# One streaming-encoder step on one core: the heads' weights loaded early, their magnitudes summed with ln_pre in the matmul, and prepared one step ahead

## The chip, the core and the metric

The kernel runs on one core of a Trainium2 chip. The metric is the device time of one execution in microseconds (us). Engines are named as the profile names them: PE is TensorE (PEld its weight loads), DVE is VectorE, ACT is ScalarE, POOL is GpSimd, SP is SyncE, which here issues the DMAs. TensorE's clock has two levels, 1.2 and 2.4 GHz; the profile's PEclk column says which share of 2.4 GHz was granted (0.5 is 1.2 GHz).

## What is computed

One layer is applied to a prompt of 4096 tokens and to a sample of 32 tokens of a running stream (model width 1024).

```
h    = RMSNorm(x) * ln_pre
proj = h @ w_in          # columns: B_a | C_a | X_a | Z_a | qkv (1536) | Z_g (512) | a_dec, b_beta (8)
q,k,v = silu(conv4_causal(qkv));  q, k L2-normalised per head (4 heads x 128)
S_t  = exp(g_t) (I - beta_t k_t k_t^T) S_{t-1} + beta_t k_t v_t^T ;  o_t = q_t^T S_t / sqrt(128)
y_g  = RMSNorm_head(o) * silu(Z_g);   y_a = B_a * conv3_causal(C_a * X_a) * silu(Z_a)
y    = x + RMSNorm_post(concat(y_a, y_g) @ w_out) * ln_post
```

## The kernel before, in words

Matmuls run on f16 pairs (a high and a low part; three products replace one f32 product). A weight column tile `ct` is 128 columns of `w_in`: 0 to 15 belong to group A, 16 to 31 to the heads (q 16 to 19, k 20 to 23, v 24 to 27, Z_g 28 to 31), and 32 holds the eight gate columns. Each tile is prepared once: it is loaded (512 KB), multiplied by `ln_pre` (line 182), its absolute values (184) are summed over the rows by eight matmuls with a matrix of ones (190), a power of two per column follows from the sum (193 to 200), the tile is scaled by it (202), and split into the high part on ACT (651) and the low part on POOL or DVE (652). Two tiles, a pair, are prepared together by `prep_b`.

The program has three stages: the heads with the sequential recurrence (to about 1320 us), group A by a Winograd scheme (to about 2000 us) and the output projection. The heads' stage goes over 16 blocks of 256 tokens; the sample goes with block 0. A block takes the eight pairs in the order k, k, q, q, v, v, z, z (`steps`); each is a projection (388 to 390, `pjs_...` for the sample, `pj_...` for the block), and for q, k and v a convolution with three DVE instructions per tile (405). Weights of the heads are prepared during block 0, the pair of a step in that step (from step 5 on, `AS`, one step ahead). Group A's tiles are prepared during the later blocks by `prep_a`, which runs after `subst` of its block, a chain of small POOL instructions (495 to 500) whose result `merge` needs (546) for the block's recurrence.

The order of the instructions on each engine's queue is set when the program is built, by a scheduler with its own clock; each queue then runs strictly in that order, and the loads of SP likewise. Tiles are loaded into a ring of five buffers, `xt`, which the loads of `x` share (k tiles go to rooms `v` and `zg`, which only later blocks fill). A load waits until its buffer's last reader is done.

Of the kernel before, what the change touches and what calls it, by code (L numbers as in the profile page):

```python
# [10 lines left out]
BF16 = mybir.dt.bfloat16  # L11
F32 = mybir.dt.float32
I32 = mybir.dt.int32
AF = mybir.ActivationFunctionType
ALU = mybir.AluOpType
# [3 lines left out]
P = 128  # L19
D = 1024  # L20
KT = D // P
NH = 4
NB1 = 256
# [9 lines left out]
NXT = 5  # L33
# [1 line left out]
LS = 2  # L35
XPE = 256
AH = 1
AS = 5
VLN = (20,)
VLO = (21,)  # L40

# [1 line left out]
def bc(ap, axis, n):  # L43

    shape = list(ap.shape)
    shape.insert(axis, n)
    return ap.unsqueeze(axis).to_broadcast(shape)
# [3 lines left out]
def hybrid_kernel(  # L51
# [11 lines left out]
    dma = nc.sync.dma_start  # L63
# [89 lines left out]
    def bank(tag, shape, nm):  # L153
        return pp.tile(shape, F32, tag=tag, bufs=1 if tag in "om" else 2, name=f"{tag}{nm}")
# [7 lines left out]
    def te(shape, dtype, tag, bufs=1, nm=""):  # L162
        return pe.tile(shape, dtype, tag=tag, bufs=bufs, name=f"{tag}{nm}")

    def tl(shape, dtype, tag, bufs=1, nm=""):
        return pl.tile(shape, dtype, tag=tag, bufs=bufs, name=f"{tag}{nm}")

    def scaled(cts, n=P, urow=None):


        ws = []
        first = cts[0] >= 16
        nm = f"{cts[0]}"
        L = bank("r" if first else "g", [P, 2, P], f"L{nm}")[:, :len(cts), :n]
        for i, ct in enumerate(cts):
            if 20 <= ct < 24:
                w = tl([P, D], F32, "v" if ct < 22 else "zg", 2, f"w{ct}")
            else:
                w = te([P, D], F32, "xt", NXT, f"w{ct}")
            w = w.rearrange("p (k c) -> p k c", k=KT)[:, :, :n]  # L180
            dma(w, w_in[:, ct * P:ct * P + n].rearrange("(k p) c -> p k c", p=P))
            (V if ct in VLN or not first else G).tensor_tensor(w, w, bc(lnp, 2, n), ALU.mult)
            ab = te([P, D], BF16, "jb", 1, f"w{ct}").rearrange("p (k c) -> p k c", k=KT)[:, :, :n]
            A.activation(ab, w, AF.Abs)
            kn = KT
            if not first:
                for kn in (4, 2, 1):
                    V.tensor_tensor(ab[:, 0:kn], ab[:, 0:kn], ab[:, kn:2 * kn], ALU.add)
            for k in range(kn):
                T.matmul(L[:, i], ones16, ab[:, k, :], start=k == 0, stop=k == kn - 1)  # L190
            ws.append(w)
        e = te([P, 2, P], I32, "we", 1, nm)[:, :len(cts), :n]
        V.tensor_scalar(e.bitcast(F32), L, 2.0 ** -100, None, ALU.max)
        V.tensor_scalar(e, e, EXP_MASK, None, ALU.bitwise_and)
        if urow is not None:
            V.tensor_scalar(urow.bitcast(I32), e[:, 0], 1, float(-(WS + HS) * BIT), ALU.mult, ALU.add)
        else:
            u = te([1, 2, P], I32, "wu", 1, nm)
            V.tensor_scalar(u, e[0:1], 1, float(-(WS + HS) * BIT), ALU.mult, ALU.add)
        V.tensor_scalar(e, e, -1, float((254 + WS) * BIT), ALU.mult, ALU.add)  # L200
        for i, w in enumerate(ws):
            V.tensor_tensor(w, w, bc(e[:, i].bitcast(F32), 1, KT), ALU.mult)
        if urow is None:
            up = bank("o" if first else "g", [P, 2], f"u{nm}")
            for i in range(2):
                T.matmul(up[:, i:i + 1], u[:, i].bitcast(F32), one1, start=True, stop=True)
            V.tensor_copy(usc[:, cts[0]:cts[0] + 2], up)
        return ws


    order = {"exp": None, "silu": None}
# [501 lines left out]
    smp = blocks1[0]  # L713
    groups[SG].insert(0, smp)
    xprep(groups[0][0])

    cst = te([P, 2, P], I32, "we", 1, "cst")[:48, 0].bitcast(F32)
    dma(cst, conv_qkv_w[0].rearrange("j (c p) -> (j c) p", p=P))
# [48 lines left out]
    for gi, grp in enumerate(groups):  # L767
        for b in grp:
            setup_block(b)
            if b["s"]:  # L770
                b["hist"] = te([P, 12, 3], F32, "hists", 2, "i")
                if gi:
                    for c in range(0, 12, 2):
                        init_hist(b, 16 + c)
                state[1] = te([P, NH, P], F32, "hl", 4, "s0")
                dma(state[1], state_gdn[0, 0].rearrange("h k v -> k h v"))
            elif gi:
                b["hist"] = groups[gi - 1][-1]["hist_new"]
        for si, (kind, c0) in enumerate(steps):
            if gi == 0 and si == 4:  # L780
                in_turn([gates(b) for b in grp])
                for b in grp:
                    decays(b)
            if gi == 0:
                for kd_, c_ in steps[:si + 1 + (AH if si >= AS else 0)]:
                    ct = (28 if kd_ == "z" else 16) + c_
                    if ct not in W:
                        prep_b(ct)
                if kind != "z":
                    init_hist(smp, 16 + c0)  # L790
            for b in grp:
                n = b["n"]
                if kind == "z":
                    z_pair(b, c0)
                elif kind == "v":
                    qkv_pair(b, c0, b["v"][:, c0 - 8:c0 - 6, :n])
                else:
                    h0 = c0 % 4
                    qkv_pair(b, c0, b["qk"][:, h0:h0 + 2, 0 if kind == "k" else 1, :n])
            finish(prevs, si)  # L800
            if si == (2 if gi else 6) and gi + 1 < len(groups):
                for b in groups[gi + 1]:
                    xprep(b)
            s1 = 4 if gi + LS < len(groups) else 3
            if si in (s1, s1 + 1):
                for b in grp:
                    if si - s1 < b["nch"]:
                        stage1(b, si - s1)
            if si == s1 + 1:
                for b in grp:  # L810
                    rnorms(b)
                    subst(b)
            if si == (3 if gi else 7) and gi + 1 < len(groups):
                in_turn([gates(b) for b in groups[gi + 1]])
            if si == 6 and 1 <= gi <= 13 or si == 2 and gi in (4, 7, 10):

                p = grp[-1] if si == 6 else prevs[-1]
                with tc.issue_after(p["stage1_end"]), tc.issue_after(p["subst_end"]):
                    prep_a()
        if gi + 1 < len(groups):  # L820
            for b in groups[gi + 1]:
                decays(b)
        for b in grp:
            if b["last"]:
                out_hist(b)
        prevs = grp
# [426 lines left out]
```

## Time and profile before

| | us |
|---|---|
| median of 3 runs (lowest, highest) | 2398.5 (2389.68, 2398.57) |
| profiled execution, its own time | 2393.51 |
| its span in the profile | 2391.8 |
| PE busy in the span | 2156.4 (90%) |
| DVE, ACT, POOL busy | 1699.0 (71%), 992.5 (41%), 1195.2 (50%) |
| mean granted clock of PE | 0.962 |

Busy shares are means over the whole span. Stretch by stretch the picture differs: PE is busy 53 to 60 us of nearly every 60 from 240 us on, and a third to three quarters of it before, during block 0. A "releaser" in a row is what ended the idle time of an engine. Times in the profile are counted from the span's start.

### The profile page before, as it was taken

Reading aid. Unit: us, or ns where it says so; the run is one execution under the profiler, and the core shown is the slowest. Engines: PE = TensorE matmul, PEld = TensorE weight load, DVE = VectorE, ACT = ScalarE, POOL = GpSimd, SP = SyncE. Lnnn points to the kernel's source line nnn. Section 1 sums busy time; section 2 is a strip of 40 time slices with the busy share of each in tenths; the row PEclk is TensorE's granted clock in tenths of the full one; section 3 lists DMA queues with packets and bytes.
Section 4 is the critical chain, followed back from the end, with each engine's and each line's share of the span. In section 5 each row is a group of like instructions: output and inputs, shape, how many; then the busy total and the mean of one; then the engine's idle time right before and its main releaser. Section 6 shows DMA issues by size and latency. Waiting matters only on the chain. (4 is left out here: it accounts for less than half of the span.)

```text
span 2391.8 us, 48652 instructions
## 1 busy us (share of the span) xinstructions
PE 2156.4 (90%) x18626; PEld 1706.8 (71%) x18626; DVE 1699.0 (71%) x4666; ACT 992.5 (41%) x2497; POOL 1195.2 (50%) x1581
## 2 busy tenths in 40 slices
PE   3677989899999999999999799899999999999998
PEld 3566877778777777787778678788888887444443
DVE  4886878987689888786777675676575565666763
ACT  4454656565666566555654220222121121433321
POOL 3526246752575644454454740766456611554542
PEclk9888999999999999999989899999999999999999
DMA  6334333534333442244324304311211133443431
GB/s 117 53 93 106 80 75 96 116 82 92 92 100 78 109 112 75 68 91 118 70 72 125 101 24 174 104 66 54 80 59 39 54 100 98 136 150 115 157 115 54
DMA packets 296913, 221.39 MB, mean 93 GB/s; under 512 B 166392, under 2 KB 236856, under 8 KB 296680
## 3 DMA queue, kind: packets, MB, share of 16 engines
q1 hardware_dynamic: 296680, 218.28, 33.5%
q8 instruction: 146, 2.39, 0.4%
q14 instruction: 87, 0.71, 0.1%
HBM read 127.84 MB, written 74.64 MB: 85 GB/s over the span
## 5 line engine op out<-in xcount | busy, mean ns | idle before, releaser
L388 PE MATMUL pj_c<-hhi,w 128*128 128x256 f16 x1536 | 429.3, 280 | 1.2 <-DMA hhi<-xth 1.2
L390 PE MATMUL pj_c<-hhi,w 128*128 128x256 f16 x1536 | 429.7, 280 | 0.0
L389 PE MATMUL pj_c<-hlo,w 128*128 128x256 f16 x1536 | 428.9, 279 | 0.0
L867 PEld LDWEIGHTS <-w_a 128*128 128x128 f16 x2880 | 269.9, 99 | 59.5 <-issue 25.6
L1130 PEld LDWEIGHTS <-opm 128*128 128x128 f16 x1536 | 149.6, 98 | 189.8 <-issue 15.5
L500 POOL TENSOR_TENSOR lt<-lt 128x112 f32<-128x112 f32 (+29 forms) x496 | 250.0, 504 | 38.9
L495 POOL TENSOR_TENSOR la<-la,lt 128x1024 f32<-128x1024 f32 x16 | 38.7, 2421 | 449.9 <-DVE lt L490 270.9
L390 PEld LDWEIGHTS <-w 128*128 128x128 f16 x2176 | 215.5, 100 | 53.2 <-POOL w L652 23.0
L499 POOL TENSOR_TENSOR lt<-la,lt 128x112 f32<-128x112 f32 (+29 forms) x496 | 233.1, 470 | 38.8
L388 PEld LDWEIGHTS <-w 128*128 128x128 f16 x2176 | 215.8, 100 | 34.1 <-issue 2.1
L389 PEld LDWEIGHTS <-w 128*128 128x128 f16 x2176 | 215.7, 100 | 30.7 <-issue 0.5
L405 DVE SCALAR_TENSOR_TENSOR qk<-u,cw,qk 128x256 f32<-128x256 f32 x384 | 214.9, 596 | 9.0 <-ACT qk L403 8.4
L867 PE MATMUL pja<-op,w_a 128*128 128x256 f16 x1536 | 194.5, 276 | 7.0 <-DVE w L881 3.4
L1079 POOL TENSOR_TENSOR mab<-mab 128x1024 bf16<-128x1024 bf16 (+2 forms) x48 | 103.6, 2159 | 130.8 <-ACT mab L1077 128.4
L867 PE MATMUL ga<-op,w_a 128*128 128x256 f16 x1152 | 149.8, 275 | 14.0 <-DVE w L881 8.1
L389 PE MATMUL pj_z<-hlo,w 128*128 128x256 f16 x512 | 144.6, 282 | 0.0
L390 PE MATMUL pj_z<-hhi,w 128*128 128x256 f16 x512 | 144.4, 282 | 0.0
L388 PE MATMUL pj_z<-hhi,w 128*128 128x256 f16 x512 | 144.3, 282 | 0.0
L1130 PE MATMUL pjo<-w_o,opm 128*128 128x512 f16 x528 | 118.2, 379 | 3.8 <-DVE v13y L1154 2.0
L1130 PE MATMUL ro<-w_o,opm 128*128 128x512 f16 x504 | 114.7, 383 | 3.9 <-DVE v7y L1154 2.0
L881 DVE TENSOR_TENSOR w<-pja,w 128x256 f32<-128x256 f32 x168 | 67.4, 420 | 70.6 <-PE pja L867 68.0
L1130 PE MATMUL go<-w_o,opm 128*128 128x512 f16 x504 | 112.7, 379 | 3.9 <-DVE v19y L1154 2.0
(707 smaller groups left out, 4946.5 us busy)
## 6 DMA issues: line engine op xcount, KB each, us to landing
xt<-in_x_prompt_dram SPq DMA_DIRECT2D x32, 512.0 KB
op<-hTd SPq DMA_DIRECT2D x32, 512.0 KB
mx<-mxd SPq DMA_DIRECT2D x16, 1024.0 KB
xtw<-in_w_in_dram SPq DMA_DIRECT2D x28, 512.0 KB
wad<-hl SPq DMA_DIRECT2D x56, 256.0 KB
gB<-gd SPq DMA_DIRECT2D x16, 516.0 KB
hTd<-hhi SPq DMA_DIRECT2D x16, 512.0 KB
hTd<-hlo SPq DMA_DIRECT2D x16, 512.0 KB
```

The lines of the kernel that those rows point to most:

```text
L388: T.matmul(pt[:, i, :n], wh[:, k, :], b["hi"][:, k, :n], start=k == 0, stop=False)
L389: T.matmul(pt[:, i, :n], wh[:, k, :], b["lo"][:, k, :n], start=False, stop=False)
L390: T.matmul(pt[:, i, :n], wl[:, k, :], b["hi"][:, k, :n], start=False, stop=k == KT - 1)
L405: V.scalar_tensor_tensor(d, u[:, i, j:j + n], cw[:, j, c0 + i:c0 + i + 1], d, ALU.mult, ALU.add)
L495: E.tensor_tensor(la, la, bc(rl, 1, 32), ALU.mult)
L499: E.tensor_tensor(tm, bc(la[:, j, j + 1:32], 2, w), bc(lt[:, j, 0:w], 1, r), ALU.mult)
L500: last = E.tensor_tensor(lt[:, j + 1:32, 0:w], lt[:, j + 1:32, 0:w], tm, ALU.subtract)
L867: T.matmul(out, lt(x, k), rh(y, k), start=start and k == n == 0, stop=stop and k == 3 and n == 2)
L881: V.tensor_tensor(dst, p, src, ALU.add)
L1079: G.tensor_tensor(ab[:, 0:m], ab[:, 0:m], ab[:, m:2 * m], ALU.add)
L1130: T.matmul(p, mo[:, x, k, t * P:t * P + m], WO[y, k][:, hf * 512:hf * 512 + 512], start=k == i == 0, stop=k == KT - 1 and i == 2)
```

## The change

- The ten tiles of the heads that are first in order (20 to 23, 16 to 19) and, two steps ahead, the others get a function `stage` that only issues the load. Tiles 16 and 17 go to a buffer of the tag `qk`, tile 18 to `la`, the gate columns to `hl`, tiles 19 and 24 on to the ring `xt`; tiles 20 to 23 stay in `v` and `zg`.
- For the heads' tiles the absolute values are taken from the weight as loaded, and the eight matmuls use the absolute values of `ln_pre`, spread to 128 columns (`lnab`, one ACT instruction at the start), as the left operand instead of ones. The multiplication by `ln_pre` stays, but the sum no longer waits for it. The absolute values go to two buffers (`o`) instead of one (`jb`).
- Pairs are prepared one step ahead from the first step (`AS` is gone), and loaded one more step ahead.
- For group A's 16 tiles the multiplication by `ln_pre` moves from DVE to POOL.

```diff
+    def stage(ct, n=P):
+        nm = f"w{ct}"
+        if ct in (20, 21, 22, 23):
+            w = tl([P, D], F32, "v" if ct < 22 else "zg", 2, nm)
+        elif ct in (16, 17):
+            if ct == 16:
+                staged["qk"] = tl([P, NH, 2, NB1], F32, "qk", 3, nm).rearrange("p h x n -> p (h x n)")
+            w = staged["qk"][:, (ct - 16) * D:(ct - 15) * D]
+        elif ct == 18:
+            w = tl([P, 32, 32], F32, "la", 1, nm).rearrange("p a b -> p (a b)")
+        elif n < P:
+            w = te([P, KT * n], F32, "hl", 4, nm)
+        else:
+            w = te([P, D], F32, "xt", NXT, nm)
+        w = w.rearrange("p (k c) -> p k c", k=KT)
+        dma(w, w_in[:, ct * P:ct * P + n].rearrange("(k p) c -> p k c", p=P))
+        staged[ct] = w
...
-            (V if ct in VLN or not first else G).tensor_tensor(w, w, bc(lnp, 2, n), ALU.mult)
-            ab = te([P, D], BF16, "jb", 1, f"w{ct}").rearrange("p (k c) -> p k c", k=KT)[:, :, :n]
-            A.activation(ab, w, AF.Abs)
...
+            w = staged.pop(ct)
+            if first:
+                ab = tl([P, D], BF16, "o", 2, f"w{ct}").rearrange("p (k c) -> p k c", k=KT)[:, :, :n]
+                A.activation(ab, w, AF.Abs)
+                (V if ct in VLN else G).tensor_tensor(w, w, bc(lnp, 2, n), ALU.mult)
+                for k in range(KT):
+                    T.matmul(L[:, i], lnab[:, k], ab[:, k, :], start=k == 0, stop=k == KT - 1)
             else:
+                G.tensor_tensor(w, w, bc(lnp, 2, n), ALU.mult)
...
+    lnab = tl([P, KT, P], BF16, "vn", 1, "lnab")
+    A.activation(lnab, bc(lnp, 2, P), AF.Abs)
...
     xprep(groups[0][0])
+    for ct in (20, 21):
+        stage(ct)
...
+    for ct in (22, 23, 16, 17, 18, 19):
+        stage(ct)
+    prep_b(22)
...
-                for kd_, c_ in steps[:si + 1 + (AH if si >= AS else 0)]:
-                    ct = (28 if kd_ == "z" else 16) + c_
+                cts = [(28 if kd_ == "z" else 16) + c_ for kd_, c_ in steps]
+                for ct in cts[:si + 1 + AH]:
                     if ct not in W:
                         prep_b(ct)
+                for ct in cts[si + 1 + AH:si + 2 + AH]:
+                    if ct not in staged:
+                        stage(ct)
+                        stage(ct + 1)
```

What this does to the queues shows in three places. On SP, at the start of the program, the kernel before issues the loads of `x` (xt), small constants (nea, dtb, gwc), the gate columns (xtw_302) and only then the second pair of k tiles:

```order
L235 DMA xt_0_238<-in_x_prompt_dram 128x1024
L235 DMA xt_128_241<-in_x_prompt_dram 128x1024
L731 DMA nea<-in_a_log_dram 128x4
L734 DMA dtb<-in_dt_bias_dram 128x4
L735 DMA gwc<-in_gdn_norm_w_dram 128x1
L181 DMA xtw_302<-in_w_in_dram 128x8x8
L776 DMA hls_332<-in_state_gdn_dram 128x4x128
L181 DMA zgw_468<-in_w_in_dram 128x8x128
L181 DMA zgw_481<-in_w_in_dram 128x8x128
L181 DMA xtw_643<-in_w_in_dram 128x8x128
```

The changed kernel, at the same place of SP's queue:

```order
L261 DMA xt_0_240<-in_x_prompt_dram 128x1024
L261 DMA xt_128_243<-in_x_prompt_dram 128x1024
L185 DMA zgw_290<-in_w_in_dram 128x8x128
L185 DMA zgw_292<-in_w_in_dram 128x8x128
L185 DMA qkw_294<-in_w_in_dram 128x8x128 x2
L185 DMA law_297<-in_w_in_dram 128x8x128
L185 DMA xtw_299<-in_w_in_dram 128x8x128
L762 DMA nea<-in_a_log_dram 128x4
L765 DMA dtb<-in_dt_bias_dram 128x4
L766 DMA gwc<-in_gdn_norm_w_dram 128x1
L185 DMA hlw_359<-in_w_in_dram 128x8x8
```

Six tile loads (22, 23, 16 to 19) moved ahead of the constants and of the gate columns, which are now hlw_359. On ACT, in block 0's first step, the kernel before takes the gate columns' absolute values (jbw_305) early, and the copies of the transposed x (hhi_235) come some rows later:

```order
L184 ACTIVATE jbw_305<-xtw_302 128x8x8
L184 ACTIVATE jbw_471<-zgw_468 128x1024
L651 ACTIVATE w_20_226<-vw_188 128x1024
L184 ACTIVATE jbw_484<-zgw_481 128x1024
L651 ACTIVATE w_21_230<-vw_201 128x1024
L248 ACTIVATE xt_0_238<-xt_0_238,xss_237 128x1024
L248 ACTIVATE xt_128_241<-xt_128_241,xss_237 128x1024
L184 ACTIVATE jbw_646<-xtw_643 128x1024
L253 ACTIVATE hhi_235<-gx_0_0_257 128x4x128
```

The changed kernel, the same stretch of ACT's queue:

```order
L274 ACTIVATE xt_128_243<-xt_128_243,xss_239 128x1024
L763 ACTIVATE nea<-nea 128x4
L202 ACTIVATE ow_361<-hlw_359 128x8x8
L202 ACTIVATE ow_525<-qkw_294 128x1024
L279 ACTIVATE hhi_237<-gx_0_0_259 128x4x128
L677 ACTIVATE w_22_336<-zgw_290 128x1024
L279 ACTIVATE hhi_237<-gx_0_1_266 128x4x128
L202 ACTIVATE ow_536<-qkw_294 128x1024
L677 ACTIVATE w_23_340<-zgw_292 128x1024
```

The gate columns (ow_361) now stand behind the scaling of x and directly ahead of x's copies. On POOL, the kernel before multiplies four further tiles by `ln_pre` before the first low part (w_20_227):

```order
L182 TENSOR_TENSOR xtw_302<-xtw_302,lnp 128x8x8
L182 TENSOR_TENSOR zgw_468<-zgw_468,lnp 128x1024
L182 TENSOR_TENSOR zgw_481<-zgw_481,lnp 128x1024
L182 TENSOR_TENSOR xtw_643<-xtw_643,lnp 128x1024
L182 TENSOR_TENSOR xtw_656<-xtw_656,lnp 128x1024
L652 TENSOR_TENSOR w_20_227<-vw_188,w_20_226 128x1024
L182 TENSOR_TENSOR xtw_818<-xtw_818,lnp 128x1024
```

The changed kernel, POOL from the same row on:

```order
L203 TENSOR_TENSOR zgw_290<-zgw_290,lnp 128x1024
L203 TENSOR_TENSOR zgw_292<-zgw_292,lnp 128x1024
L678 TENSOR_TENSOR w_20_229<-vw_184,w_20_228 128x1024
L203 TENSOR_TENSOR hlw_359<-hlw_359,lnp 128x64
L203 TENSOR_TENSOR qkw_294<-qkw_294,lnp 128x1024
L678 TENSOR_TENSOR w_22_337<-zgw_290,w_22_336 128x1024
L203 TENSOR_TENSOR qkw_294<-qkw_294,lnp 128x1024
```

The first low part no longer stands behind the loads of tiles 16 and 17, and the gate columns stand between it and the rest.

## Rows read from the trace of the kernel before

**Rows 1.** Windows of 60 us: length, busy us per engine, PEclk, DMA share, GB/s

```profile
0.00:60.00 60.00, 22.06 (x236) 18.78 (x237) 24.65 (x86) 24.59 (x37) 21.86 (x27) 0.99 0.60 117
60.00:120.00 60.00, 40.10 (x467) 32.90 (x464) 49.12 (x106) 28.40 (x49) 30.50 (x15) 0.81 0.35 52
120.00:180.00 60.00, 44.95 (x467) 36.90 (x468) 52.58 (x191) 30.82 (x95) 15.94 (x13) 0.80 0.41 97
240.00:300.00 60.00, 57.72 (x562) 48.78 (x560) 50.48 (x164) 37.92 (x101) 14.68 (x21) 1.00 0.32 80
```

**Rows 2.** Waits of PE before 180 us: total us, times, longest

```profile
PE rL L190 <- ACT jbw L184: 26.8, 7, 13.4
PE pjs_c L390 <- POOL w L652: 21.9, 5, 8.5
```

**Rows 3.** Timeline of PE: start, us; two projections of block 0 and 1, a wait

```profile
45.49 0.38 PE L388 MATMUL pj_c<-hhi,w 128*128 128x256 f16 x1
...
159.62 2.07 PE L442 MATMUL gq<-qk 128*128 128x256 f32 x4 [4.58 <-DVE kd L431]
...
171.95 0.27 PE L388 MATMUL pj_c<-hhi,w 128*128 128x256 f16 x1 [1.19 <-DMA hhi<-xth]
```

**Rows 4.** POOL's groups from 0 to 172 us: count | busy, mean ns | idle before

```profile
L652 POOL TENSOR_TENSOR w<-xtw,w 128x1024 f16<-128x1024 f32 x12 | 26.6, 2228 | 4.0 <-ACT w L651 4.0
L182 POOL TENSOR_TENSOR xtw<-xtw,lnp 128x1024 f32<-128x1024 f32 (+1 forms) x13 | 24.3, 1868 | 58.5 <-DMA xtw<-in_w_in_dram 58.5
```

**Rows 5.** Windows, columns as in rows 1

```profile
26.00:172.00 146.00, 94.43 (x1040) 77.40 (x1040) 109.63 (x300) 73.76 (x162) 60.97 (x36) 0.84 0.38 68
...
64.00:151.00 87.00, 57.82 (x651) 47.12 (x650) 73.32 (x186) 45.72 (x99) 41.48 (x21) 0.78 0.36 64
```

**Rows 6.** DVE's groups from 64 to 151 us, shapes kept apart

```profile
L405 DVE SCALAR_TENSOR_TENSOR qk<-u,cw,qk 128x256 f32<-128x256 f32 x20 | 12.5, 661 | 4.8 <-ACT qk L403 4.8
L405 DVE SCALAR_TENSOR_TENSOR qks<-us,cw,qks 128x32 f32<-128x32 f32 x18 | 7.6, 451 | 0.0
L405 DVE SCALAR_TENSOR_TENSOR vss<-us,cw,vss 128x32 f32<-128x32 f32 x12 | 6.2, 550 | 0.0
L405 DVE SCALAR_TENSOR_TENSOR v<-u,cw,v 128x256 f32<-128x256 f32 x12 | 5.4, 467 | 0.0
```

**Rows 7.** Line 405 before 172 us: ns min/median/max, first and last start

```profile
L405 DVE SCALAR_TENSOR_TENSOR qks<-us,cw,qks x24: 232/244/2161, 48.0 to 109.1; 128x32 f32<-128x32 f32 x24
```

**Rows 8.** Timeline of DVE and POOL at 118 us

```profile
118.10 4.27 POOL L652 TENSOR_TENSOR w<-xtw,w 128x1024 f16<-128x1024 f32 x2 [1.50 <-ACT w L651]
...
118.24 2.06 DVE L310 SCALAR_TENSOR_TENSOR gus<-gus,gexs 32x4 f32<-32x4 f32 x1
...
120.29 2.10 DVE L309 COPY beta<-ru 128x8 f32<-128x8 f32 x1
...
122.31 0.15 DVE L310 SCALAR_TENSOR_TENSOR gu<-gu,gex 128x8 f32<-128x8 f32 x1
```

**Rows 9.** Timeline of DVE: scaling of tiles 16 and 17, and of 30 and 31

```profile
63.98 2.34 DVE L202 TENSOR_TENSOR xtw<-xtw,we 128x1024 f32<-128x1024 f32 x2
...
151.11 2.36 DVE L202 TENSOR_TENSOR xtw<-xtw,we 128x1024 f32<-128x1024 f32 x2
```

**Rows 10.** DMA from 0 to 40 us, all queues

```profile
DMA packets 10872, 5.25 MB, mean 131 GB/s; under 512 B 2742, under 2 KB 10583, under 8 KB 10871
```

**Rows 11.** Timeline of ACT: gate columns; a whole tile; a copy of x

```profile
20.03 0.25 ACT L184 ACTIVATE jbw<-xtw 128x64 bf16<-128x64 f32 x1
...
26.68 1.06 ACT L184 ACTIVATE jbw<-zgw 128x1024 bf16<-128x1024 f32 x1 [6.40 <-POOL zgw L182]
27.64 1.04 ACT L651 ACTIVATE w<-vw 128x1024 f16<-128x1024 f32 x1
...
45.70 0.60 ACT L253 ACTIVATE hhi<-gx 128x512 f16<-128x512 f32 x1 [0.26 <-PE gx L252]
```

**Rows 12.** POOL's start of subst, whole span, columns as in rows 4

```profile
L495 POOL TENSOR_TENSOR la<-la,lt 128x1024 f32<-128x1024 f32 x16 | 38.7, 2421 | 449.9 <-DVE lt L490 270.9
```

**Rows 13.** Line 182 on DVE after block 0: ns min/median/max, first and last start

```profile
L182 DVE TENSOR_TENSOR xtw<-xtw,lnp x16: 1215/1219/1220, 270.2 to 1105.8; 128x1024 f32<-128x1024 f32 x16
```

More of the change, by code (lines that the diff above doesn't have):

```diff
@@ L37 @@
 AH = 1
-AS = 5
 VLN = (20,)
@@ L166, in tl @@
         return pl.tile(shape, dtype, tag=tag, bufs=bufs, name=f"{tag}{nm}")
+    staged = {}
+    def stage(ct, n=P):
[15 more added lines that the diff above has]
+        staged[ct] = w
     def scaled(cts, n=P, urow=None):
@@ L174, in scaled @@
         L = bank("r" if first else "g", [P, 2, P], f"L{nm}")[:, :len(cts), :n]
+        for ct in cts:
+            if ct not in staged:
+                stage(ct, n)
         for i, ct in enumerate(cts):
-            if 20 <= ct < 24:
-                w = tl([P, D], F32, "v" if ct < 22 else "zg", 2, f"w{ct}")
-            else:
-                w = te([P, D], F32, "xt", NXT, f"w{ct}")
-            w = w.rearrange("p (k c) -> p k c", k=KT)[:, :, :n]
-            dma(w, w_in[:, ct * P:ct * P + n].rearrange("(k p) c -> p k c", p=P))
-            (V if ct in VLN or not first else G).tensor_tensor(w, w, bc(lnp, 2, n), ALU.mult)
-            ab = te([P, D], BF16, "jb", 1, f"w{ct}").rearrange("p (k c) -> p k c", k=KT)[:, :, :n]
-            A.activation(ab, w, AF.Abs)
-            kn = KT
-            if not first:
+            w = staged.pop(ct)
[5 more added lines that the diff above has]
+                    T.matmul(L[:, i], lnab[:, k], ab[:, k, :], start=k == 0, stop=k == KT - 1)
+            else:
+                G.tensor_tensor(w, w, bc(lnp, 2, n), ALU.mult)
+                ab = te([P, D], BF16, "jb", 1, f"w{ct}").rearrange("p (k c) -> p k c", k=KT)[:, :, :n]
+                A.activation(ab, w, AF.Abs)
                 for kn in (4, 2, 1):
                     V.tensor_tensor(ab[:, 0:kn], ab[:, 0:kn], ab[:, kn:2 * kn], ALU.add)
-            for k in range(kn):
-                T.matmul(L[:, i], ones16, ab[:, k, :], start=k == 0, stop=k == kn - 1)
+                T.matmul(L[:, i], ones16, ab[:, 0, :], start=True, stop=True)
             ws.append(w)
@@ L784, in hybrid_kernel @@
             if gi == 0:
-                for kd_, c_ in steps[:si + 1 + (AH if si >= AS else 0)]:
-                    ct = (28 if kd_ == "z" else 16) + c_
+                cts = [(28 if kd_ == "z" else 16) + c_ for kd_, c_ in steps]
+                for ct in cts[:si + 1 + AH]:
                     if ct not in W:
                         prep_b(ct)
+                for ct in cts[si + 1 + AH:si + 2 + AH]:
+                    if ct not in staged:
+                        stage(ct)
+                        stage(ct + 1)
                 if kind != "z":
```

## The prediction

> **What bounds the kernel now.** I read the windows first. From 240 us on PE is busy nearly all the time (57.7 of 60 us in the window shown); in the first three windows it is not (22, 40 and 45 of 60), and there its granted clock falls to about 0.8, that is, part of the time at 1.2 GHz [rows 1]. All that the change does to the heads' weights lies in this beginning. Block 0 ends where PE starts on block 1, at 171.95 us [rows 3]; a gain there is handed on, since PE works without long gaps behind it. Next the waits of PE in this stretch: the two largest are for the absolute values of a weight tile (26.8 us) and for its low part from POOL (21.9 us) [rows 2]. POOL's groups say why the low part is late: POOL itself waited 58.5 us for loads of tiles [rows 4]. This is the wait that the change attacks.
>
> The next view keeps me from counting it all as gain. From 26 to 172 us DVE is busy 109.6 of 146 us, so only 36.4 us of that stretch are open on DVE; POOL is busy 61.0 [rows 5]. And DVE's time is not all work. At 118 us two low parts run on POOL for 4.27 us; in that time two DVE instructions of 32 or 128 rows and a few columns take 2.06 and 2.10 us, and a like one right behind takes 0.15 [rows 8]. They end when a POOL instruction ends. So DVE and POOL, for many of their instructions, run one at a time.
>
> How much of DVE's time is such waiting? Between 64 and 151 us: 20 of the 128x256 convolution steps take 0.661 us in the mean, 12 others of that shape 0.467 [rows 6]: 20 x 0.194 = 3.9. The 128x32 steps have a median of 0.244 [rows 7]; 18 at 0.451 and 12 at 0.550 make 3.7 and 3.7 [rows 6]. The two of rows 8 add 1.9 each. That is 15.1 us, a floor, since most small groups are not in it; the ceiling is POOL's 41.5 us in that stretch [rows 5]. I take the middle, 28 (an estimate). Then DVE's own work there is 73.3 - 28 = 45.3, and with POOL's 41.5 it is 86.8 of 87.0 us: the stretch is as long as both engines one after the other.
>
> **The change part by part.** Sums are made against the profiled execution, 2393.5 us with a span of 2391.8; the median of the runs, 2398.5, is 5.0 above it.
>
> *Early loads.* POOL's wait of 58.5 us goes for the largest part. What is late next: the gate columns. Their load now stands behind ten loads of 0.5 MB in SP's queue, or 0.13 + 2 x 0.52 + 2 x 0.52 + 6 x 0.52 MB = 5.4 MB with x and the sample; in the first 40 us 5.25 MB were moved [rows 10], so it lands at about 38 us (36 to 41), where the kernel before had it at 20 [rows 11]. ACT's instruction on it stands ahead of the copies of x and of the high parts of tiles 22 and 23, and POOL's ahead of tile 16, so both queues stand from about 29 to 38 us. From there ACT needs 0.25 + 4 x 1.06 (absolute values and high parts of whole tiles) + 2 x 0.6 (copies), 43.7 us, then further absolute values and the second copies, until block 0's x is whole at about 46 us: no earlier than before, when the first projection of block 0 began at 45.5 [rows 3]. The gain so far is that tiles 22, 23, 16 and 17 are further on by then.
>
> *Scaling, pair by pair.* Tiles 16 and 17 were scaled at 64.0 us and tiles 30 and 31 at 151.1, five pairs later: 17.4 us a pair [rows 9]. In the changed order the scaling of 16 and 17 stands behind the copies' low parts (47 us) and some 20 small DVE instructions, 5 us by themselves, with two or three collisions of 2 us: 57 us, 7 earlier. A pair is then DVE's 45.3 / 5 = 9.1 us and four POOL instructions, 2 x 1.87 + 2 x 2.23 = 8.2 [rows 4]: 17.3 if they exclude each other wholly, 13.2 if half of POOL's time falls on DVE instructions that don't mind (those that read PSUM). Tiles 30 and 31 are scaled at 57 + 5 x 13.2 = 123 to 57 + 5 x 17.3 = 143.5, which is 8 to 28 us earlier. The cadence measured, 17.4, lies at the exclusive end, so I take 15, nearer to that end than to the other.
>
> *The end of block 0.* PE waits there for DVE's kd (4.58 us, until 159.62) and needs 12.3 us more to block 1 [rows 3]. This chain (gates, their way through DRAM, decays) is not shortened, and it comes later in DVE's order than the last scaling, so it may keep part of the 15 us, at the worst all; on the other side more of the Z projections are then done before kd, which gives some of those 12.3 back, at the best all. I count the two as nothing.
>
> *Absolute values from the raw tile.* They no longer wait for POOL; the 26.8 us of rows 2 are the same idle time of PE as the low parts' and are not counted a second time. The count of matmuls stays (eight a tile, 128 in all); their left operand is loaded as often as ones was. One ACT instruction is added at the start, no longer than a whole tile's 1.06 us [rows 11], under the first load. Cover gone, it costs 1.06.
>
> *Group A's tiles.* 16 x 1.22 = 19.5 us leave DVE [rows 13], 16 x 1.87 = 30 us come to POOL [rows 4]. They stand between one subst and the next, where POOL sits idle 449.9 / 16 = 28 us [rows 12]. A pair's 3.7 us fits. If each held up a DVE instruction for its whole length, DVE would have 30 back for the 19.5 it gave; PE, which is full there [rows 1], sees neither. I take nothing; the ends are a gain of 5 and a loss of 30, the latter a rival below.
>
> Sum: 2393.5 - 15 = 2378.5 against the profiled execution, 2383.5 on the scale of the runs' median. The three runs spread by 9 us, and I name 2381.
>
> The Trainium skill, in "SBUF — State Buffer", section "SBUF: two separate sides", says that DVE and GpSimd share one pair of ports under an exclusive lock: whichever starts first holds it for its whole instruction and the other fully blocks. The trace agrees where rows 8 show 2.06 us for 0.15. By that rule taken wholly the pair takes 17.3 us, and the sum would be the second rival's.
>
> **The rivals.**
> *Much larger.* Collisions don't grow, because POOL's work was there before too, and DVE's open time goes: 36.4 - 8 for the new wait up to 38 us = 28, or all 36 if the gate columns overtake the tiles. For it: POOL's 58.5 us. Against: DVE used POOL's waits to run undisturbed. 2365.5 to 2357.5.
> *No change.* DVE and POOL exclude each other wholly and the gates' chain keeps the rest: 0 to 8 us, 2385.5 to 2393.5 (2391 to name one). For it: 86.8 of 87.0 us. Against: DVE's 13.7 us idle in that same stretch [rows 5], some of it behind late tiles.
> *Slower.* In eight blocks group A's pair delays subst on POOL, subst delays merge, and merge PE: 8 x 3.7 = 30 us. It decides where POOL is idle less than 3.7 us before subst. Against: 28 us in the mean. With the forecast's 15 gained: 2408.
> That the loads don't start at once, because they queue behind each other, is in the 38 us already.
>
> **How the numbers follow.** What a measurement of this kernel can tell from no change is 0.5%, 12 us. The likeliest case (8 to 22 us gained, 2371 to 2390) gets 0.52, the larger gain 0.15, no change 0.24, slower 0.09. Of the likeliest, four fifths lie over 12 us: faster 0.42 + 0.15 = 0.57; same 0.10 + 0.24 = 0.34; slower 0.09. The range goes from the larger gain's 2358 to no change on the median's scale, 2398; it leaves out most of the slower case and some of each end.
>
> **What would show it.** Right: PE's first projection of block 1 at 150 to 164 us; POOL's wait for loads under 20 us before then; ACT's instruction on the gate columns at 36 to 41 us with both queues idle before it; more DVE instructions of 2 us, per us, between 45 and 130; the idle time before subst down by about 4 us in eight blocks without a longer wait of merge. Wrong: block 1 at 140 us or earlier (collisions matter less than I say), at 166 or later (they or the gates' chain eat it all), or block 1 early and the later stages longer by as much.

## The result, and the profile after

The changed kernel takes 2514.0 us (median of four runs, 2510.4 to 2534.5), the kernel before, in runs beside it, 2394.1: a ratio of 1.052 (95% interval 1.049 to 1.056), 120 us slower. The profiled execution has a span of 2508.5 us and a mean granted clock of 0.933 where the kernel before had 0.962. The prediction, 2381 in a range of 2358 to 2398, was wrong, on its sign too.

Where is the time? First the windows. The beginning is little changed (compare [rows 1]; columns as there):

```profile
0.00:60.00 60.00, 16.58 (x166) 14.22 (x167) 22.40 (x65) 23.64 (x32) 24.40 (x27) 1.00 0.72 130
60.00:120.00 60.00, 42.52 (x500) 35.05 (x499) 56.35 (x125) 27.74 (x51) 34.00 (x16) 0.85 0.28 57
120.00:180.00 60.00, 46.59 (x473) 38.57 (x472) 48.70 (x172) 35.44 (x102) 13.30 (x12) 0.84 0.32 84
240.00:300.00 60.00, 58.77 (x545) 49.66 (x542) 44.57 (x156) 34.00 (x102) 12.44 (x23) 1.00 0.32 80
...
300.00:360.00 60.00, 37.18 (x342) 30.62 (x343) 35.71 (x103) 25.43 (x64) 21.03 (x48) 0.74 0.34 76
540.00:600.00 60.00, 38.59 (x353) 33.10 (x351) 41.46 (x104) 23.63 (x48) 34.95 (x70) 0.78 0.34 74
840.00:900.00 60.00, 42.98 (x397) 36.98 (x398) 36.07 (x116) 32.74 (x90) 8.09 (x15) 0.75 0.40 87
1080.00:1140.00 60.00, 35.75 (x342) 30.30 (x340) 32.77 (x86) 24.00 (x47) 29.23 (x65) 0.72 0.32 71
```

The last four rows are new. In these windows PE works 36 to 43 of 60 us at a granted clock of 0.72 to 0.78, so part of the time at 1.2 GHz. The kernel before in the same windows:

```profile
300.00:360.00 60.00, 52.90 (x466) 43.22 (x467) 45.31 (x146) 31.45 (x87) 28.85 (x67) 0.91 0.38 76
540.00:600.00 60.00, 58.74 (x567) 50.57 (x566) 42.20 (x136) 32.85 (x99) 16.97 (x27) 0.97 0.41 92
840.00:900.00 60.00, 55.43 (x519) 48.16 (x519) 53.69 (x152) 34.92 (x91) 30.25 (x46) 1.00 0.47 109
1080.00:1140.00 60.00, 57.30 (x525) 47.53 (x526) 43.89 (x130) 35.01 (x88) 27.88 (x42) 0.92 0.42 111
```

There PE works 52.9 to 58.7 us, at 0.91 to 1.00. Three to four blocks lie between one such hole and the next.

Second, block 1. Its first projection starts here, where [rows 3] had 171.95:

```profile
172.40 0.27 PE L414 MATMUL pj_c<-hhi,w 128*128 128x256 f16 x1
```

The beginning gained nothing. Third, the waits of PE, first before 180 us (compare [rows 2]), then from 195 to 1442 us, which is the heads' stage from block 0's subst to the last one (total us, times, longest):

```profile
PE rL L205 <- ACT ow L202: 24.1, 5, 10.9
PE pj_c L414 <- ACT u L425: 23.1, 4, 7.4
PE gcst L759 <- DMA wecst<-in_cache_conv_qkv_dram: 11.2, 1, 11.2
PE gcss L352 <- DVE g3s L347: 5.3, 1, 5.3
...
PE m L572 <- DMA Tc<-ltd: 64.8, 25, 15.3
PE om L651 <- DVE o L648: 38.2, 17, 5.5
PE gcs L352 <- DVE g L347: 22.5, 6, 7.2
PE pj_c L414 <- ACT zg L438: 20.8, 4, 5.3
```

The same stage of the kernel before, from 189 to 1321 us:

```profile
PE m L546 <- DMA Tc<-ltd: 25.4, 17, 3.0
...
PE gcs L326 <- DVE g L321: 11.2, 7, 3.7
PE om L625 <- DVE o L622: 9.4, 13, 1.4
```

All four waits of the second list have grown: merge's for its matrix `Tc` by 39 us, with stalls of up to 15 us where there were 3, that for `o` by 29, that for the gates' `g` by 11, and a block's first projection now waits 5.2 us, four times, for `zg`. The forecast's sum had none of them at a price; its slower rival had merge's alone.

One of the four holes, read from the changed kernel's timelines of POOL, ACT and PE (start, us, engine, line; the bracket is the idle time before and its releaser):

```profile
285.84 2.37 POOL L521 TENSOR_TENSOR la<-la,lt 128x1024 f32<-128x1024 f32 x1 [53.12 <-DVE lt L516]
...
318.61 0.20 POOL L526 TENSOR_TENSOR lt<-lt 128x8 f32<-128x8 f32 x1
318.77 4.73 POOL L207 TENSOR_TENSOR xtw<-xtw,lnp 128x1024 f32<-128x1024 f32 x2
323.44 0.31 POOL L517 MEMSET lt<- 128x256 f32 x1
...
378.62 2.36 POOL L521 TENSOR_TENSOR la<-la,lt 128x1024 f32<-128x1024 f32 x1 [54.28 <-DVE so L117]
...
322.83 1.04 ACT L209 ACTIVATE jbw<-xtw 128x1024 bf16<-128x1024 f32 x1
326.42 1.06 ACT L209 ACTIVATE jbw<-xtw 128x1024 bf16<-128x1024 f32 x1 [2.55 <-PE gL L212]
...
335.29 1.76 ACT L700 ACTIVATE hl<-xtw 128x512 f16<-128x512 f32 x3 [2.48 <-DVE xtw L224]
...
343.79 0.82 ACT L438 ACTIVATE zg<-pj_z,usc 128x256 f32<-128x256 f32 x2
...
325.23 0.31 PE L572 MATMUL m<-Tc,M 32*32 32x32 f32 x2 [11.19 <-DMA Tc<-ltd]
...
344.66 0.37 PE L414 MATMUL pj_c<-hhi,w 128*128 128x256 f16 x1 [5.18 <-ACT zg L438]
```

POOL begins subst at 285.8 and ends it at 318.8. Only then come group A's two multiplies, which in the kernel before DVE did at 270.2 [rows 13]. Their tiles had been ordered at 195.7, and POOL was idle for 53 us before 285.8; nothing but their place in line kept them. And they hold up no subst: the next one starts at 378.6, after 54 us of idleness. What they hold up is everything behind them in other lines: ACT's absolute values (322.8 and 326.4), the sum on PE, the scaling, three copies of high parts on ACT (335.3), and behind these, in ACT's line, the gates' functions and the silu of the last Z projection (343.8) that frees the bank for the next block's first projection (344.7). All that falls on the border between two blocks, when PE has already run out of projections. In this hole it works 11.0 of 32 us, at a clock of 0.56:

```profile
313.00:345.00 32.00, 11.02 (x116) 8.80 (x117) 19.74 (x57) 17.19 (x30) 9.91 (x24) 0.56 0.60 129
```

Most of PE's 21 idle us in this hole are another wait: 12.5 are merge's for `Tc`, 11.2 of them at 325.2. Its path is the end of subst (318.8), two DMAs that SP issues at 320.3 and 323.1, and merge; the pair does not stand in it. At the same border of the kernel before subst ends at 319.6, and merge waits 2.8 us (SP of the changed kernel, then PE of the kernel before):

```profile
320.30 0.52 SPq L529 DMA_DIRECT2D ltd<-lt  x1
...
323.11 4.61 SPq L536 DMA_DIRECT2D Tc<-ltd  x8
...
326.62 0.31 PE L546 MATMUL m<-Tc,M 32*32 32x32 f32 x2 [2.84 <-DMA Tc<-ltd]
...
331.20 0.39 PE L388 MATMUL pj_c<-hhi,w 128*128 128x256 f16 x1
```

There the Z projections reach to 321.4 (to 312.6 in the changed kernel), and the next block's first projection follows at 331.2 (at 344.7). So PE stands still because its own line holds no projection at that place. How the late pair thins out PE's line was not followed; nor why only four of the eight pairs behind a subst come with such a hole.

That this order of POOL is in the program and no accident of timing shows in its queue. The kernel before, rows between two substs:

```order
L499 TENSOR_TENSOR lt_3175<-la_3174,lt_3175 128x8
L500 TENSOR_TENSOR lt_3175<-lt_3175 128x8
L491 MEMSET lt_4226 128x256
L493 MEMSET lt_4226 32x8 x4
L495 TENSOR_TENSOR la_4225<-la_4225,lt_4226 128x1024
```

and the changed kernel:

```order
L525 TENSOR_TENSOR lt_3176<-la_3175,lt_3176 128x8
L526 TENSOR_TENSOR lt_3176<-lt_3176 128x8
L207 TENSOR_TENSOR xtw_3315<-xtw_3315,lnp 128x1024
L207 TENSOR_TENSOR xtw_3317<-xtw_3317,lnp 128x1024
L517 MEMSET lt_4227 128x256
```

The program prepares a group A pair with `issue_after(p["subst_end"])`, that is, the scheduler may not issue it before the last instruction of the block's own subst. On DVE that binds nothing at run time (the multiply ran at 270.2, 13 us before subst began). On POOL, which runs subst itself, it puts the multiply behind it.

### The profile page after: what moved, and what is told of

It is laid out like the page before. It is cut to its first block, busy times and chain, and to the rows that moved or that the text cites. A ratio compares the mean times of both kernels' runs of the same rounds, so it can differ in the third digit from the quotient of the medians.

```text
span 2508.5 us, 48736 instructions
## 1 busy us (share of the span) xinstructions
PE 2176.1 (87%) x18626; PEld 1736.7 (69%) x18626; DVE 1713.5 (68%) x4650; ACT 997.3 (40%) x2498; POOL 1185.3 (47%) x1597
## 5 line engine op out<-in xcount | busy, mean ns | idle before, releaser
L414 PE MATMUL pj_c<-hhi,w 128*128 128x256 f16 x1536 | 433.1, 282 | 44.8 <-ACT u L425 23.1
L521 POOL TENSOR_TENSOR la<-la,lt 128x1024 f32<-128x1024 f32 x16 | 39.3, 2455 | 522.0 <-DVE lt L516 233.5
L1165 PEld LDWEIGHTS <-opm 128*128 128x128 f16 x1536 | 149.2, 98 | 188.6 <-issue 13.2
L526 POOL TENSOR_TENSOR lt<-lt 128x112 f32<-128x112 f32 (+29 forms) x496 | 229.9, 463 | 38.8
L525 POOL TENSOR_TENSOR lt<-la,lt 128x112 f32<-128x112 f32 (+29 forms) x496 | 211.0, 425 | 38.8
L414 PE MATMUL pj_z<-hhi,w 128*128 128x256 f16 x512 | 147.0, 287 | 0.4 <-ACT u L425 0.4
L416 PE MATMUL pj_z<-hhi,w 128*128 128x256 f16 x512 | 146.9, 287 | 0.0
```

What stands on the lines that cost most here:

```text
L414: T.matmul(pt[:, i, :n], wh[:, k, :], b["hi"][:, k, :n], start=k == 0, stop=False)
L416: T.matmul(pt[:, i, :n], wl[:, k, :], b["hi"][:, k, :n], start=False, stop=k == KT - 1)
L521: E.tensor_tensor(la, la, bc(rl, 1, 32), ALU.mult)
L525: E.tensor_tensor(tm, bc(la[:, j, j + 1:32], 2, w), bc(lt[:, j, 0:w], 1, r), ALU.mult)
L526: last = E.tensor_tensor(lt[:, j + 1:32, 0:w], lt[:, j + 1:32, 0:w], tm, ALU.subtract)
L1165: T.matmul(p, mo[:, x, k, t * P:t * P + m], WO[y, k][:, hf * 512:hf * 512 + 512], start=k == i == 0, stop=k == KT - 1 and i == 2)
```

## The experiments

The theories when they began: theory 1, it is this place in POOL's line; rival 2, the early part of the change pushes the later schedule about; rival 3, POOL's 16 multiplies cost by their load and by their clashes with DVE, wherever they stand. All results, with two marks from POOL's timeline: when the sixth subst begins, and how long it is from there to the sixteenth (ten blocks). "Block 1" is its first projection on PE. Each ratio is to runs of the kernel before beside it, whose median was 2391.0 to 2397.2.

| run | median us | ratio to before (95%) | sixth subst | ten blocks | block 1 |
|---|---|---|---|---|---|
| before | 2394.1 | 1 | 580.9 | 740.9 | 171.95 |
| after | 2514.0 | 1.052 (1.049, 1.056) | 641.1 | 801.8 | 172.40 |
| e1_dve | 2433.1 | 1.015 (1.011, 1.018) | 582.5 | 773.8 | 173.92 |
| e2_before_pool | 2504.8 | 1.043 (1.040, 1.047) | 639.2 | 788.6 | 169.01 |
| e3_ahead | 2439.4 | 1.016 (1.013, 1.019) | 592.6 | 781.8 | 175.91 |
| e4_noearly | 2503.6 | 1.043 (1.040, 1.046) | 646.2 | 790.2 | 175.37 |
| e5_small_first | 2446.7 | 1.022 (1.020, 1.024) | 592.5 | 777.6 | 173.55 |
| e6_lnab_only | 2437.2 | 1.018 (1.016, 1.020) | 584.6 | 772.3 | 174.66 |
| e7_loads_only | 2457.2 | 1.027 (1.025, 1.029) | 617.6 | 770.2 | 180.24 |
| e8_ahead_only | 2438.5 | 1.019 (1.015, 1.022) | 597.5 | 771.7 | 176.05 |
| e9_room | 2425.4 | 1.014 (1.012, 1.017) | 575.3 | 775.2 | 174.75 |
| e10_same_order | 2411.6 | 1.008 (1.006, 1.010) | 597.0 | 747.1 | 171.20 |
| e11_same_order_b | 2399.7 | 1.002 (1.001, 1.004) | 581.6 | 741.5 | 170.23 |
| e12_loads | 2421.5 | 1.011 (1.009, 1.014) | 599.3 | 744.4 | 173.35 |
| e13_no_next | 2418.0 | 1.011 (1.008, 1.013) | 595.5 | 744.0 | 173.24 |
| e14_ones | 2411.5 | 1.008 (1.006, 1.010) | 590.8 | 747.3 | 178.02 |
| e15_cache_last | 2422.5 | 1.013 (1.011, 1.016) | 601.8 | 744.2 | 173.97 |

**The multiply: four runs.** *e1_dve*, from the changed kernel:

```diff
-                G.tensor_tensor(w, w, bc(lnp, 2, n), ALU.mult)
+                V.tensor_tensor(w, w, bc(lnp, 2, n), ALU.mult)
                 ab = te([P, D], BF16, "jb", 1, f"w{ct}")...
```

> The changed kernel with group A's ln_pre multiply back on VectorE, nothing else undone. Theory 1 (on POOL the multiply stands in line behind the subst of its own block, so the pair's absolute values, sums and scaling come only when subst ends, at the block's border, and ACT, DVE and PE stand there): the heads' stage ends at about 1320 us again, 2380 to 2400 us in all. Rival 2 (the early loads and the other new order in the beginning push the later schedule about): the loss stays, 2490 to 2515. Rival 3 (POOL's 16 multiplies cost by their load on POOL and on the ports shared with DVE, wherever they stand): 2380 to 2400, as theory 1.

*e2_before_pool*, from the kernel before:

```diff
-            (V if ct in VLN or not first else G).tensor_tensor(w, w, bc(lnp, 2, n), ALU.mult)
+            (V if ct in VLN else G).tensor_tensor(w, w, bc(lnp, 2, n), ALU.mult)
```

> The kernel before with one thing changed: group A's ln_pre multiply on POOL instead of VectorE. Theory 1: 2490 to 2515 us, with four long stalls of PE at borders of blocks, as in the changed kernel. Rival 2: as before, 2390 to 2400. Rival 3: 2490 to 2515, as theory 1.

*e3_ahead*, from the changed kernel: `mult_a` loads the next pair and multiplies it on POOL, and `scaled` then leaves the multiply out for it.

```diff
+            if si == 4 and gi in (1, 3, 4, 6, 7, 9, 10, 12):
+                with tc.issue_after(prevs[-1]["subst_end"]):
+                    mult_a()
```

> The changed kernel, group A's multiply still on POOL, but issued two steps earlier in the program, ahead of the block's subst (it has to follow the subst of the block before). Sums, absolute values and scaling stay where they were. Theory 1: POOL does the pair in its idle time ahead of subst, 2385 to 2410 us. Rival 2: 2490 to 2515. Rival 3: 2490 to 2515, since POOL does the same work.

*e4_noearly*, from the changed kernel, without the loops that call `stage` ahead and without `prep_b(22)` in the beginning:

```diff
-                for ct in cts[:si + 1 + AH]:
+                for ct in cts[:si + 1 + (AH if si >= AS else 0)]:
```

> The changed kernel without its early part: no tile is loaded ahead, pairs are prepared ahead only from step 5 as in the kernel before; ln_pre as left operand, absolute values of the raw tile and group A's multiply on POOL stay. Theory 1: still 2490 to 2520 us. Rival 2: 2390 to 2410. Rival 3: 2490 to 2520.

The multiply back on DVE takes 81 us off the changed kernel (2514.0 to 2433.1). The multiply alone, put on POOL in the kernel before, adds 108 (2397.2 to 2504.8, side by side). Left on POOL but put ahead of subst, it costs 6 us against DVE, which is inside the spread of the two runs, and the long waits for `Tc` are gone: the longest in the heads' stage is 15.3, 12.4 and 18.1 us where the pair stands behind subst (*after*, *e2*, *e4*) and 3.8 in *e1*. The waits of PE in *e3_ahead* from 186 to 1430 us begin with:

```profile
PE om L653 <- DVE o L650: 32.0, 16, 4.9
PE gcs L354 <- DVE g L349: 29.0, 7, 8.8
PE m L574 <- DMA Tc<-ltd: 25.5, 12, 4.6
```

So theory 1 holds for the larger part, and rival 3 falls: the engine was not the fault, its line was. But *e1_dve* and *e3_ahead* lie 33 and 29 us above what theory 1 expected of them, and both are slower than the kernel before. Rival 2 owns a share. And 81 and 108 hold more than the one wait: where the pair moves, the scheduler orders the other lines anew too, and no run kept those lines and moved the multiply alone.

**Which part of the rest? Four runs**, all with group A's multiply on DVE. *e5_small_first* is *e1_dve* with these lines moved ahead of eight large loads (two of `x` and tiles 22, 23, 16 to 19; the tiles that the change loads early are these six and 20 and 21, eight and not ten):

```diff
+    cst2 = te([P, 2, P], I32, "we", 1, "cst2")[:36, 0].bitcast(F32)
+    dma(cst2, cache_conv_qkv[0, 0].rearrange("j (c p) -> (j c) p", p=P))
...
+    stage(32, 8)
     if SG == 0:
         xprep(groups[0][1])
     for ct in (22, 23, 16, 17, 18, 19):
         stage(ct)
```

> As the run with group A's multiply back on VectorE, and the load of the convolution cache and of the gate columns issued ahead of eight of the ten tiles. Theory A (the 36 us that are still lost come from those two small loads, which land some 10 to 25 us late, and the later stages only hand it on): 2385 to 2410 us. Rival B (they come from the other new order and stay): 2415 to 2435.

*e6_lnab_only* is *e4_noearly* with the edit of *e1_dve*. *e7_loads_only* and *e8_ahead_only* are *e1_dve* with one half of the early part undone each (in *e7* the loop over `cts` as in *e4* and no early `prep_b(22)`; in *e8* no early `stage`).

> The kernel before with one part of the change: absolute values of the raw tile, summed with the absolute ln_pre as left operand (and tiles 16 to 18 in other rooms), no load ahead, preparation ahead only from step 5, group A's multiply on VectorE. If this part costs the 36 us: 2425 to 2440. Theory A and B: 2385 to 2405.

> As the run with group A's multiply on VectorE, with the early loads but the preparation as in the kernel before (one step ahead only from step 5). Theory A: the small loads are late here too, 2420 to 2440. Rival B, if the earlier preparation is what reorders the rest: 2385 to 2405.

> As the run with group A's multiply on VectorE, with the preparation one step ahead but no load issued ahead of its pair. Theory A: 2385 to 2410, since the small loads don't stand behind ten tiles. Rival B: 2420 to 2440.

In *e5* half of the edit took effect. The gate columns come early (ACT takes them at 23.0 us, at 40.7 in the changed kernel). The cache's load does not; on SP it still stands behind the tiles, 14.5 us later than in the kernel before (31.0), and PE waits 16.7 us for it:

```profile
45.51 3.10 SPq L752 DMA_DIRECT2D wecst<-in_cache_conv_qkv_dram  x1
```

None of the four goes back to 2394: whichever part is left in, 43 to 63 us are lost, and in the ten blocks, where the code of all of them is that of the kernel before, each takes 770 to 778 us instead of 741. Theory A fails by that, whatever the small loads do: it has the later stages only hand a loss on, and here the ten blocks lose 29 to 37 us themselves. Rival B fails in *e6* and *e7*, which it expected at 2385 to 2405. No part is to blame by itself, and a new theory is needed. What the four share is that the queues of the heads' stage come out in another order: the scheduler works with a clock of its own, and an edit of the beginning can shift what it finds ready later. *e1* and *e6*, one with early loads and one without, even have the same order on DVE, ACT, POOL and SP from the fifth subst on, but for one row; their ten blocks take 773.8 and 772.3 us.

**Is it the order? Three runs.** *e9_room* is the kernel before with one tile of 32 KB in another ring:

```diff
-                w = te([P, D], F32, "xt", NXT, f"w{ct}")
+                w = te([P, D], F32, "xt", NXT, f"w{ct}") if n == P else te([P, KT * n], F32, "hl", 4, f"w{ct}")
```

> The kernel before with one neutral edit: the gate columns' tile (128 x 64) lies in another ring of buffers. No work is added or moved to another engine, but the scheduler, which orders the queues as the program is built, comes to another order of the heads' stage from the second block on. Theory S (the 36 to 60 us that remain without group A's multiply are the price of leaving the order that the kernel before has in the heads' stage, whatever edit leaves it): 2425 to 2460 us. Rival P (the parts themselves cost it): 2390 to 2400.

*e10_same_order* and *e11_same_order_b* are *e1_dve* with small edits of rooms (`elif n < 0`, so the gate columns lie in the ring `xt`; *e10* also has the convolution cache's load first in the program, as in *e5* but without `stage(32, 8)`; on SP it stands at 44.1 us, behind the early tiles; *e11* keeps the one buffer `jb` for the absolute values). With these the rows of DVE, ACT, POOL and SP stand in the order of the kernel before, but for a row or two, from ahead of the sixth subst to the end of the heads' stage.

> The changed kernel with group A's multiply on VectorE, the gate columns in the ring of the kernel before, and the convolution cache loaded ahead of eight of the ten tiles. All else of the change stays (ten early loads, one step ahead, ln_pre as left operand, absolute values of the raw tile). On DVE, ACT, POOL and SP the rows from the second block on stand in the order of the kernel before. Theory S: 2375 to 2400 us, with a gain of up to 15 us in block 0 if the end of the block lets it through. Rival P: 2425 to 2445.

> As the run before this one in the list, but the convolution cache stays behind the tiles, as in the changed kernel, and the absolute values lie in one buffer. The heads' stage again has the order of the kernel before. Theory S: 2385 to 2405 us, later than the other by the wait for the convolution cache (6 to 11 us). Rival P: 2425 to 2445.

A neutral edit costs 32 us, and almost the whole change, in the old order, costs 6.5 us. Block by block *e11* runs as before: 741.5 us for the ten blocks against 740.9. Theory S holds there; in *e10*, which missed its 2375 to 2400, the ten blocks take 747, and 16 of the 24 us by which its profiled execution is longer are lost ahead of the sixth subst.

Theory S says more than that, namely that leaving the old order costs, whatever edit leaves it, and this does not hold everywhere. Between the first and the fifth subst roughly 300 of DVE's 755 rows stand in another place in *e11* than in the kernel before, and at the sixth it is level (581.6 against 580.9). And *e9* and *e1* lose their time between the sixth and the ninth subst (*e9* goes from 5.6 us ahead of the kernel before to 28.5 behind, *e1* from 1.6 to 34.7 behind) and nothing from there to the sixteenth, in an order that still is not the old one. So another order can be as good as the old; these are worse in places.

A worse order shows on DVE. The same ten blocks in the kernel before, in *e11*, in *e9* and in *e1* (one row each; third busy figure is DVE's, fifth POOL's):

```profile
580.00:1321.00 741.00, 686.58 (x6387) 582.39 (x6386) 585.71 (x1796) 423.08 (x1159) 405.99 (x746) 0.96 0.38 95
```

```profile
581.00:1323.00 742.00, 689.13 (x6407) 586.01 (x6406) 586.68 (x1799) 423.13 (x1157) 405.78 (x746) 0.96 0.38 95
```

```profile
575.00:1350.00 775.00, 702.26 (x6481) 594.72 (x6479) 617.25 (x1813) 428.76 (x1171) 410.26 (x746) 0.96 0.38 92
```

```profile
582.00:1356.00 774.00, 697.53 (x6484) 592.20 (x6483) 613.41 (x1818) 428.28 (x1168) 412.46 (x746) 0.97 0.38 92
```

Nearly the same number of instructions keep DVE busy 28 to 32 us longer, and the stretch is 33 to 34 us longer. PE is busy 11 to 16 us longer too; that DVE's longer work is what lengthens the stretch is likely, not shown. The largest share lies in one group, the 120 convolution steps of `v` (the kernel before, then *e9*; count | busy us, mean ns):

```profile
L405 DVE SCALAR_TENSOR_TENSOR v<-u,cw,v 128x256 f32<-128x256 f32 x120 | 59.8, 531 | 1.3 <-ACT v L403 1.0
```

```profile
L405 DVE SCALAR_TENSOR_TENSOR v<-u,cw,v 128x256 f32<-128x256 f32 x120 | 73.4, 651 | 1.8 <-ACT v L403 1.4
```

Those of the 120 that overlap no POOL instruction take 0.48 us in both kernels, those that do 0.57 in the kernel before and 0.86 in *e9*. The rest is spread over many groups. One instruction, in *e9* (timelines of DVE and POOL): a step on 128x2 numbers, 0.16 us in the median, takes 2.21 and ends when subst's first multiply ends, which began 0.17 us before it.

```profile
575.27 0.16 DVE L118 SCALAR_TENSOR_TENSOR xss<-xss 128x2 f32<-128x2 f32 x1
575.47 2.21 DVE L119 SCALAR_TENSOR_TENSOR xss<-xss 128x2 f32<-128x2 f32 x1
...
575.30 2.35 POOL L495 TENSOR_TENSOR la<-la,lt 128x1024 f32<-128x1024 f32 x1 [32.51 <-DVE xss L117]
```

The Trainium skill, in "SBUF — State Buffer", section "Who interferes with whom", says that the order of issue, and not the shape of the operation, decides who blocks. The trace agrees: the same DVE step is short or long (0.16 or 2.21 us) by what POOL has begun.

**Does the beginning gain anything in the old order? Four runs.** Each has some of the early part, in an arrangement that keeps the order of the heads' stage (from ahead of the sixth subst on). *e12* is the kernel before with this early list and the cache's load ahead of its second part in the program; nothing is loaded or prepared further ahead:

```diff
+    for ct in (20, 21):
+        stage(ct)
...
+    for ct in (22, 23, 16, 17, 18):
+        stage(ct)
```

*e14* has neither tile 18 nor 19 in the list, but loads the later tiles two steps ahead and prepares pairs one step ahead; both sum with ones after the multiply, as before. The other two are nearly the whole change, other than their expectations say: eight tiles are loaded early and the later ones two steps ahead. *e15_cache_last* is *e11_same_order_b* without one line, so that the pair 22, 23 is no longer prepared in the beginning:

```diff
-    prep_b(22)
```

*e13_no_next* is *e10_same_order* without the same line and with the one buffer `jb`.

> The kernel before with early loads of seven tiles (20 to 23, 16 to 18) in unused room and the convolution cache ahead of five of them; sums with ones as before, preparation ahead only from step 5, group A's multiply on VectorE, heads' stage in the order of the kernel before. Theory E (block 0 ends with the gates' chain, which no early tile shortens): block 1 at 170 to 174 us, 2388 to 2400 us. Rival L (early loads gain when the small loads come first): block 1 at 156 to 166, 2375 to 2388.

> Early loads of seven tiles, convolution cache first, preparation one step ahead, ln_pre as left operand; no later tile is loaded ahead of its pair. Group A's multiply on VectorE, heads' stage in the order of the kernel before. Theory E: block 1 at 170 to 176 us, 2390 to 2412. Rival L: block 1 at 156 to 166, 2375 to 2388.

> Early loads of six tiles (20 to 23, 16, 17), convolution cache first, one step ahead, sums with ones as before; heads' stage in the order of the kernel before. Theory E: block 1 at 170 to 176 us, 2390 to 2405. Rival L: block 1 at 156 to 166, 2375 to 2388.

> Early loads of seven tiles, convolution cache behind them, one step ahead, ln_pre as left operand; heads' stage in the order of the kernel before. Theory E: block 1 at 170 to 176 us, 2390 to 2405. Rival L: 2385 to 2395, behind the run with the cache first by some 5 us.

Block 1 begins where theory E said in three of the four (173.2 to 174.0 us; in *e14* at 178.0, 2 us beyond). Rival L is not refuted by that. It asks that the small loads come first, and in none of the runs do they: on SP the cache's load stands at 41.9 to 44.9 us whether the program has it first or last, 31.0 in the kernel before, and ACT takes the gate columns at 40.8 to 43.3, 20.0 there. The nearest to it is *e5*, with the gate columns early and the cache late, and its block 1 begins at 173.55. No version starts block 1 before 169 us.

But all four are 20 to 32 us slower than the kernel before, 6 to 21 us beyond the top of what theory E expected. Their ten blocks take 744 to 747; most of the rest is lost ahead of the sixth subst (590.8 to 601.8 against 580.9), where the order of rows differs from the kernel before. It differs in *e11* too, which loses nothing there: the one line between *e11* and *e15* is worth 20 us at the sixth subst (581.6 and 601.8) and 23 us in all. Which rows there cost it was not followed up. No version beats the kernel before.

## Why the prediction was wrong, point by point

- **"Group A's tiles ... A pair's 3.7 us fits ... I take nothing."** This step failed, and it is the largest: 81 us in the changed kernel, 108 in the kernel before alone. I counted the length of the work (3.7 us; it is 3.75 to 4.73) against POOL's idle time in the mean [rows 12], and never asked on which side of subst the pair stands. The idle time lies ahead of subst; the pair comes behind it (318.8 us, on DVE 270.2).
- **The slower rival** had the right part of the change, the wrong mechanism and the wrong size. It let the pair delay subst by 3.7 us in eight blocks. The pair does not delay subst: before it POOL now idles 522.0 us where it had 449.9. The pair itself is late, ACT, DVE and PE stand in line behind it, and PE's line has no projections left at that place.
- **"A gain there is handed on"** takes for granted that from block 1 on the kernel would run as before. The stage was ordered anew, and *e9_room* shows that this alone can cost 32 us. All rows from 180 us on that I used were rows of an order that the change does away with.
- **Early loads**: right in what goes, wrong in what comes instead. POOL no longer waits for loads of tiles before 172 us (58.5 us in [rows 4]). In their place it waits 33.2 us for ACT's absolute values and 23.9 for ACT's high parts (4.0 before). PE's wait for low parts (21.9 us, [rows 2]) is gone, that for absolute values is not (24.1, 26.8 before), and 23.1 us for ACT's `u` have come; ACT for its part waits 24.6 us for DVE's convolution steps (2.4 before). The gate columns were foreseen (5.4 MB at the 131 GB/s of [rows 10] are 41 us and not 38; ACT takes them at 40.73). Missed is the convolution cache: its load, small as it is, comes at 50.0 us on SP and PE waits 11.2 us for it, DVE with it.
- **"86.8 of 87.0"** was no finding. It follows from the 28 us in the middle between the floor and the ceiling; with the floor, 15.1, the sum is 99.7, with the ceiling 73.3. And the clock of about 0.8 is that of the second and third window; the first has 0.99 [rows 1].
- **Scaling, pair by pair**: the pace came inside the 13.2 to 17.3 us expected, the start late. The pairs are scaled from 63.46 (57 was expected) to 139.08 us, five pairs in 75.6, 15.1 us each, 17.4 before [rows 9]. So the last pair is 12 us earlier, where 15 was taken:

```profile
63.46 1.22 DVE L224 TENSOR_TENSOR qkw<-qkw,we 128x1024 f32<-128x1024 f32 x1
...
139.08 1.21 DVE L224 TENSOR_TENSOR xtw<-xtw,we 128x1024 f32<-128x1024 f32 x1
```

- **The end of block 0, counted at nothing**: this is the second step that failed. It took back the whole 12 us by which the last pair was earlier (151.1 to 139.1). PE waits until 147.19 for the sample's gates (`g3s`), 5.3 us, with the Z projections behind it in line; in the kernel before the same wait ends at 124.3. So the chain of the gates, which "is not shortened", came 23 us later. In 16 variants block 1 begins at 169 to 180 us. From 80 to 172 us DVE is busy 79.1 us in the kernel before, 81.8 in the changed one and 88.9 in *e11*, of 92. What sets the end of the block in all of them stays open.
- **DVE and POOL one at a time** [rows 8]: held for many instructions, here and in the later stage. The q and k steps of 128x256 between 45 and 130 us take 791 ns in the mean; in the same window of the kernel before it was 629.

Sum: of the 117 us between the two spans, 60 are lost up to the sixth subst, 61 in the next ten blocks, and the last stages give back 4. By experiment, 81 are the place of the multiply with what it does to the other lines; of the other 36 to 39 (*e1*), 33 lie in the ten blocks and go with the order.

## What to carry to other kernels

Before work moves to another engine, read what will stand ahead of it in that engine's queue, and who waits behind it in other queues: an idle share in the mean says nothing about the place. Where a scheduler orders the queues, an edit can reorder the stages that it does not touch; compare the order there first, and measure a neutral edit to learn how much the order alone is worth (here 1.4%). And look at each queue before reading a run: a line moved to the front of the program, like the cache's load, need not come first on its engine.

## What was not expected of the hardware

The same DVE work, in another order against POOL's, keeps DVE busy 28 to 32 us longer in ten blocks; the 120 convolution steps of `v` alone have 13.6 of them, and single steps of 0.16 us take 2.2. And a hole on PE also slows the work in it and next to it: in the one shown the granted clock was 0.56 over 32 us, after 1.00 just before, and it is 0.86 over the 10 us behind it, in which PE works without a break.
